# A pair's two heads: the six score products of an attention front multiplied in turn, head by head

## The chip, the cores and the metric

The kernel runs on one core of a Trainium2 chip. The metric is the device time of one execution in microseconds (us). Engines are named as in the profile: PE (TensorE, matrix products), PEld (its weight loads), DVE (VectorE), ACT (ScalarE), POOL (GpSimd), SP (the queue that issues the transfers).

## What is computed

One step of a hybrid encoder layer for 1024 prompt rows and 32 sample rows, width 2048, float32. One input projection feeds four branches; the change touches branch B, stick-breaking attention with 8 heads of width 64. For each block of 128 queries:

```python
z = jnp.einsum('bqhd,bkhd->bhqk', qblk, k).astype(jnp.float32) * scale
mask = (k_pos[None, :] < pblk[:, None])[None, None]
log_keep = jnp.where(mask, jax.nn.log_sigmoid(-z), 0.0)
suffix = lax.cumsum(log_keep, axis=3, reverse=True) - log_keep
w = jnp.where(mask, jnp.exp(jax.nn.log_sigmoid(z) + suffix), 0.0)
return jnp.einsum('bhqk,bkhd->bqhd', w, v32)
```

## The kernel before

The 1024 prompt rows are worked in two halves, h = 0 (with the 32 sample rows) and h = 1. The input projection goes through 48 column tiles of 128 (`col_tile`, L363 to L365): a tile `ip` is summed over 16 slices, with three products each, because a float32 operand is split into a high and a low part (`wh`, `wl` for weights, `uh`, `ul` for the input). A product streams 272 or 274 columns in half 0 and 512 in half 1 (256 twice where a half is cut in two). Weights come by SP (`wr`), ACT casts the high part (L338), DVE subtracts the low part (L339).

Branch B works on four pairs of heads, p = 0 to 3, in `b_unit`. A pair's q and k lie transposed in one tile each: head j = 0 in partitions 0 to 63, head j = 1 in 64 to 127. After the projections of q, k and v it runs 4 fronts in half 0 (query blocks i = 0 to 3 against the keys of this half up to the diagonal: 256, 256, 384 and 512 columns) and 8 in half 1 (the same four, and for each query block one more against the 512 keys of half 0, `prev`). That is 16 + 32 = 48 fronts. A front computes, for each of the two heads, the scores `z` as three products (high by high L737, high by low L738, low by high L739), each of which contracts over the head's 64 rows: on the array this is the form 64*128, where the projection has 128*128. Then `stick` lets ACT take two sigmoids of `z` (`s` L709, `kp` L710); POOL masks the diagonal block; DVE scans `kp` and multiplies (L718, L722). A later turn transposes the weights on PE (`turned`, `wt` L834) and multiplies them by the values (`values`, `av` L849, form 128*64).

`z` lies in PSUM in a pool of two buffers, so that a front's first head takes the buffer of the last front's first head and may be written when ACT's `kp` of that head is done; likewise the second head.

What runs around a front is set in two places. Python generators are woven: after so many steps of a projection tile, the next step of an attention unit is written out (`weave`, the table `ORDER`). Then a scheduler lists each engine's instructions in a fixed order, by its own estimate of when operands and buffers are ready; work under `tc.high_priority()` goes ahead of other work that is ready. `behind(a, b)` binds instruction a to stand behind b on its engine, without a wait. Engines carry out their list in this order.

Of the kernel before, what the change touches and what calls it, by code (L numbers as in the profile page):

```python
# [13 lines left out]
P = 128  # L14
# [48 lines left out]
def step_kernel(ctx, tc, xp, xs, cst, wmss, wmg, bgate, win, wsm, wout, lng, lnb, ck, cv,  # L63
# [19 lines left out]
    def nm(s):  # L83
        uid[0] += 1
        return f"{s}_{uid[0]}"

    def IO(s="io"):
        return io.tile([P, SLOT], F32, tag="io", name=nm(s))

    def WK(s="wk", shape=None):  # L90
        return wk.tile(shape or [P, SLOT], F32, tag="wk", name=nm(s))

    def ZT(s="z"):
        return ps_z.tile([P, 512], F32, tag="z", name=nm(s))
# [16 lines left out]
    T = nc.tensor  # L111
# [85 lines left out]
    def behind(ins, other):  # L197

        if other is not None:
            tc.add_manual_dep(ins.ins, other.ins.name, mybir.DependencyInfo(  # L200
                mybir.DependencyClass.NoSync, mybir.DependencyReason.DATA), reason="order")
        return ins
# [501 lines left out]
    def stick(z, rows, nk, diag, carry):  # L704


        s = WK("s")
        kp = WK("kp")
        A.activation(s[0:rows, 0:nk], z, AF.Sigmoid, scale=QSCALE)  # L709
        A.activation(kp[0:rows, 0:nk], z, AF.Sigmoid, scale=-QSCALE)  # L710
        if diag is not None:
            diag(s, kp)
        pr = WK("pr")
        init = 1.0
        if carry is not None:
            A.copy(pr[0:rows, nk:nk + 1], carry[0:rows, 0:1])
            init = carry[0:rows, 0:1]
        V.tensor_tensor_scan(pr[0:rows, 0:nk][:, ::-1], kp[0:rows, 0:nk][:, ::-1], kp[0:rows, 0:nk][:, ::-1],  # L718
                             initial=init, op0=ALU.mult, op1=ALU.bypass)

        m = nk - 1 if carry is None else nk
        V.tensor_tensor(s[0:rows, 0:m], s[0:rows, 0:m], pr[0:rows, 1:m + 1], op=ALU.mult)  # L722
        return s, pr
# [3 lines left out]
    def parts(t, name, n=512):  # L727

        th = io.tile([P, 512], F32R, tag="io", name=nm(name + "h"))
        tl = io.tile([P, 512], F32R, tag="io", name=nm(name + "l"))  # L730
        A.copy(th, t[:, 0:n])
        V.tensor_tensor(tl, t[:, 0:n], th.bitcast(F32), op=ALU.subtract)
        return th, tl

    def products(out, x, y, start, stop):

        T.matmul(out, x[0], y[0], start=start, stop=False)  # L737
        T.matmul(out, x[0], y[1], start=False, stop=False)  # L738
        T.matmul(out, x[1], y[0], start=False, stop=stop)  # L739
# [14 lines left out]
    def b_unit(h, p):  # L754
        n = 544 if h == 0 else 512
        tt = {}
        for name, tid in (("q", T_Q + p), ("k", T_K + p), ("v", T_V + p)):
            res = yield from col_tile(h, tid)
            t = IO(name)
# [11 lines left out]
        qs, ks_ = parts(q, "q"), parts(k, "k")  # L771
# [26 lines left out]
        if h == 1:  # L798
            prev_ = []
            for src in (ksc, vsc):  # L800
                t = (WK if src is ksc else IO)("prev")
# [4 lines left out]
        def front(i, st, kk, m, dg):  # L806

            def diag(s, kp):
                b = slice(i * P, (i + 1) * P)
                G.affine_select(out=s[:, b], in_=s[:, b], pattern=[[-1, P]], compare_op=ALU.is_gt,  # L810
                                fill=0.0, base=0, channel_multiplier=1)
                G.affine_select(out=kp[:, b], in_=kp[:, b], pattern=[[-1, P]], compare_op=ALU.is_gt,  # L812
                                fill=1.0, base=0, channel_multiplier=1)

            w = []
            for j in range(2):
                d = slice(64 * j, 64 * j + 64)
                z = ZT("z")
                products(z[:, 0:max(m, 256)], [t[d, i * P:(i + 1) * P] for t in qs],
                         [t[d, 0:max(m, 256)] for t in kk], True, True)  # L820
                wj, st[j] = stick(z[:, 0:m], P, m, diag if dg else None, st[j])
                w.append(wj)
            return w

# [33 lines left out]
        for i in range(4):  # L858
            st = [None, None, None]
            keys = [(ks_, vt, P * (i + 1), True)]  # L860
            if h == 1:
                keys.append((*prev_, 512, False))
            for x, (kk, vv, m, dg) in enumerate(keys):
                w = front(i, st, kk, m, dg)
                if todo2:
                    values(*todo2)
                    todo2 = None
                if todo1:
                    todo2 = (*todo1[:2], turned(todo1[2], todo1[4]), *todo1[3:])
                todo1 = (i, st, w, vv, m, x == 0, x == len(keys) - 1)  # L870
                yield 1
# [774 lines left out]
```

## Time and profile before

| | |
|---|---|
| time, median of 3 runs | 1991.29 us (1990.73 to 1994.05) |
| the profiled execution, its own time | 1989.37 us |
| its span, first to last instruction | 1987.6 us |
| mean granted TensorE clock | 0.984 |
| PE busy | 1901.5 us |
| DVE busy | 1338.2 us |
| ACT busy | 773.8 us |

The page gives the busy time of each engine over the span, and the views give single instructions with start and length. Matrix products overlap on PE, so the length of one says less than the distance from its start to the start of the next; that distance is called a step below. The rows of the timeline merge instructions of one line that follow each other (x2 is two of them).

### The profile page before, as it was taken

How to read it: one execution, taken by the hardware profiler on the slowest of the kernel's cores; microseconds unless marked ns; L12 is line 12 of the kernel's file. 1: busy time of each engine (PE TensorE's matmuls, PEld its weight loads, DVE VectorE, ACT ScalarE, POOL GpSimd, SP SyncE). 2: the span in 40 equal slices, each digit the busy share in tenths (PEclk: the TensorE clock that was granted, in tenths of full speed). 3: DMA queues.
4: the chain of work that ended last, by engine and by line, in shares of the span. 5: the costliest groups of instructions: out<-in, count | busy, mean ns of one | idle time of the engine just before them, and what ended most of it. 6: DMA issues, size and time to landing. Idle time of an engine off the chain costs nothing. (4 is left out here: it accounts for less than half of the span.)

```text
span 1987.6 us, 31999 instructions
## 1 busy us (share of the span) xinstructions
PE 1901.5 (96%) x12194; PEld 1578.5 (79%) x12194; DVE 1338.2 (67%) x2573; ACT 773.8 (39%) x1288; POOL 301.2 (15%) x505
## 2 busy tenths in 40 slices
PE   4999999999999999999999999999999999998997
PEld 2678999998898999876788786777878667676787
DVE  4425577977967858777677969875756653455765
ACT  5212433334564434544444444433345421133321
POOL 1100112212112202441101102021113310000000
PEclk9899999999999999998999999999999999999998
DMA  9787344333453343633233332332334554557633
GB/s 344 249 290 235 105 127 136 111 125 119 146 166 121 104 130 98 183 130 114 95 114 100 103 126 68 117 111 94 126 102 141 162 167 138 172 182 238 212 129 133
DMA packets 162098, 291.42 MB, mean 147 GB/s; under 512 B 23900, under 2 KB 66140, under 8 KB 161944
## 3 DMA queue, kind: packets, MB, share of 16 engines
q1 hardware_dynamic: 161944, 289.37, 45.2%
q8 instruction: 96, 1.57, 0.3%
q14 instruction: 58, 0.48, 0.1%
HBM read 253.49 MB, written 35.82 MB: 146 GB/s over the span
## 5 line engine op out<-in xcount | busy, mean ns | idle before, releaser
L363 PE MATMUL ip<-uh,wh 128*128 128x272 f32 (+3 forms) x2304 | 759.1, 330 | 0.7 <-POOL uh L288 0.7
L364 PE MATMUL ip<-ul,wh 128*128 128x272 f32 (+3 forms) x2304 | 747.4, 324 | 0.0
L365 PE MATMUL ip<-uh,wl 128*128 128x272 f32 (+3 forms) x2304 | 745.7, 324 | 0.0
L338 ACT CAST wh<-wr 128x1024 fp32r<-128x1024 f32 x253 | 264.0, 1044 | 635.3 <-PE ip L364 362.9
L339 DVE TENSOR_TENSOR wl<-wr,wh 128x1024 fp32r<-128x1024 f32 x253 | 312.1, 1235 | 240.1 <-ACT wh L338 222.5
L363 PEld LDWEIGHTS ip<-uh,wh 128*128 128x128 f32 x2304 | 438.7, 190 | 42.0 <-issue 9.6
L365 PEld LDWEIGHTS ip<-uh,wl 128*128 128x128 f32 x2304 | 438.2, 190 | 35.7 <-issue 4.5
L364 PEld LDWEIGHTS ip<-ul,wh 128*128 128x128 f32 x2304 | 438.2, 190 | 32.9 <-issue 4.3
L1256 PE MATMUL op<-wh,yh 128*128 128x512 f32 (+1 forms) x576 | 216.6, 376 | 7.8 <-DVE val L1267 7.8
L1258 PE MATMUL op<-wh,yl 128*128 128x512 f32 (+1 forms) x576 | 216.5, 377 | 0.0
L1257 PE MATMUL op<-wl,yh 128*128 128x512 f32 (+1 forms) x576 | 215.5, 374 | 0.0
L1118 DVE SCALAR_TENSOR_TENSOR cv<-cin,cs,cv 128x574 f32<-128x574 f32 (+1 forms) x240 | 187.5, 781 | 2.8
L1256 PEld LDWEIGHTS op<-wh,yh 128*128 128x128 f32 x576 | 109.4, 190 | 31.4 <-DVE val L1267 8.6
L1258 PEld LDWEIGHTS op<-wh,yl 128*128 128x128 f32 x576 | 109.3, 190 | 26.8 <-issue 7.2
L1257 PEld LDWEIGHTS op<-wl,yh 128*128 128x128 f32 x576 | 109.4, 190 | 24.0 <-issue 4.4
L1171 DVE SCALAR_TENSOR_TENSOR gacc<-wg,cs,gacc 128x512 f32<-128x512 f32 x120 | 91.6, 783 | 14.7 <-DMA wg<-in_wmg_dram 14.6
L810 POOL TENSOR_SCALAR_AFFINE_SELECT s<-s 128x128 f32<-128x128 f32 x64 | 37.9, 592 | 417.5 <-ACT s L709 417.1
L718 DVE TENSOR_TENSOR_SCAN pr<-kp 128x128 f32<-128x128 f32 (+4 forms) x66 | 53.9, 816 | 15.5 <-POOL kp L812 12.7
L213 PE MATMUL mod<-wmr,cpad 128*32 128x512 f32 x256 | 40.0, 703 | 25.2 <-DMA wmr<-in_wmss_dram 25.2
L709 ACT ACTIVATE s<-z 128x512 f32<-128x512 f32 (+3 forms) x96 | 47.7, 497 | 36.2 <-PE z L739 34.4
L722 DVE TENSOR_TENSOR s<-s,pr 128x512 f32<-128x512 f32 (+5 forms) x106 | 59.2, 562 | 2.1 <-DVE pr L718 0.5
L1072 POOL TENSOR_TENSOR dn<-dn,mhalf 128x1 f32<-128x1 f32 (+1 forms) x36 | 27.8, 771 | 211.6 <-DVE dn L1071 207.9
(384 smaller groups left out, 2333.2 us busy)
## 6 DMA issues: line engine op xcount, KB each, us to landing
wr<-in_win_dram SPq DMA_DIRECT2D x192, 512.0 KB
wmr<-in_wmss_dram SPq DMA_DIRECT2D x128, 256.0 KB
wr<-in_wout_dram SPq DMA_DIRECT2D x63, 512.0 KB
wg<-in_wmg_dram SPq DMA_DIRECT2D x64, 256.0 KB
x<-in_xp_dram SPq DMA_DIRECT2D x32, 256.0 KB
out_dram<-val SPq DMA_DIRECT2D x32, 256.0 KB
xr<-in_xp_dram SPq DMA_DIRECT2D x28, 256.0 KB
yf<-ysc SPq DMA_DIRECT2D x16, 272.0 KB
```

The costliest lines, as they stand in the source:

```text
L338: A.copy(wh, wr)
L339: V.tensor_tensor(wl, wr, wh.bitcast(F32), op=ALU.subtract)
L363: T.matmul(pt[:, 0:n], wh[:, k % 8, :], uh[:, c0:c0 + n], start=(k == 0), stop=False)
L364: T.matmul(pt[:, 0:n], wh[:, k % 8, :], ul[:, c0:c0 + n], start=False, stop=False)
L365: T.matmul(pt[:, 0:n], wl[:, k % 8, :], uh[:, c0:c0 + n], start=False, stop=(k == KD - 1))
L718: V.tensor_tensor_scan(pr[0:rows, 0:nk][:, ::-1], kp[0:rows, 0:nk][:, ::-1], kp[0:rows, 0:nk][:, ::-1], initial=init, op0=ALU.mult, op1=AL ...
L722: V.tensor_tensor(s[0:rows, 0:m], s[0:rows, 0:m], pr[0:rows, 1:m + 1], op=ALU.mult)
L1118: V.scalar_tensor_tensor(acc[:, 0:n], t[:, i:i + n], C("cdw", 31 * j + i), acc[:, 0:n], op0=ALU.mult, op1=ALU.add)
L1171: V.scalar_tensor_tensor(acc[j][:, 0:512], wr[:, 0:512], cT[:, k, j:j + 1], acc[j][:, 0:512], op0=ALU.mult, op1=ALU.add)
L1256: T.matmul(acc[t][:, 0:w], yh[:, c], wh, start=(first and i == 0), stop=False)
L1257: T.matmul(acc[t][:, 0:w], yh[:, c], wl, start=False, stop=False)
L1258: T.matmul(acc[t][:, 0:w], yl[:, c], wh, start=False, stop=(last and i == len(ws) - 1))
```

## The change

Before, `front` took a `z` buffer for head 0, issued its three products and its `stick`, then did the same for head 1. Now it takes both buffers first, then issues six products in the order high by high of head 0, of head 1, high by low of head 0, of head 1, low by high of head 0, of head 1. Each is bound behind the one before it, and the six stand under high priority. The two `stick` calls follow. The products themselves, their sizes and the number of buffers are the same.

```diff
+            zs = [ZT("z") for _ in range(2)]
+            n = max(m, 256)
+            after = None
+            with tc.high_priority():
+                for x, (a, b) in enumerate(((0, 0), (0, 1), (1, 0))):
+                    for j in range(2):
+                        d = slice(64 * j, 64 * j + 64)
+                        after = behind(T.matmul(zs[j][:, 0:n], qs[a][d, i * P:(i + 1) * P], kk[b][d, 0:n],
+                                                start=x == 0, stop=x == 2), after)
             w = []
             for j in range(2):
-                d = slice(64 * j, 64 * j + 64)
-                z = ZT("z")
-                products(z[:, 0:max(m, 256)], [t[d, i * P:(i + 1) * P] for t in qs],
-                         [t[d, 0:max(m, 256)] for t in kk], True, True)
-                wj, st[j] = stick(z[:, 0:m], P, m, diag if dg else None, st[j])
+                wj, st[j] = stick(zs[j][:, 0:m], P, m, diag if dg else None, st[j])
                 w.append(wj)
             return w
```

The lists of the engines change with it. First PE in half 1, second pair, the front i = 2 against its own half's keys; before, the six products stood in one piece between the end of a projection tile and the values of an older front:

```order
L365 MATMUL ip_12032<-uh_9968,wl_12023 128x512
L737 MATMUL z_12057<-kh_11665,qh_11661 128x384
L738 MATMUL z_12057<-kl_11666,qh_11661 128x384
L739 MATMUL z_12057<-kh_11665,ql_11662 128x384
L737 MATMUL z_12072<-kh_11665,qh_11661 128x384
L738 MATMUL z_12072<-kl_11666,qh_11661 128x384
L739 MATMUL z_12072<-kh_11665,ql_11662 128x384
L849 MATMUL av_12087<-wt_11982,vt_11675 64x128 x4
```

In this list the head (z_12057, z_12072) changes once. The same front on PE's list of the changed kernel, where L823 is the line of all six products:

```order
L364 MATMUL ip_11917<-ul_9929,wh_11907 128x512
L823 MATMUL z_12057<-kh_11665,qh_11661 128x384
L365 MATMUL ip_11917<-uh_9928,wl_11908 128x512
L363 MATMUL ip_11917<-uh_9936,wh_11907 128x512
L364 MATMUL ip_11917<-ul_9937,wh_11907 128x512
L365 MATMUL ip_11917<-uh_9936,wl_11908 128x512
L823 MATMUL z_12058<-kh_11665,qh_11661 128x384
L823 MATMUL z_12057<-kl_11666,qh_11661 128x384
L823 MATMUL z_12058<-kl_11666,qh_11661 128x384
L823 MATMUL z_12057<-kh_11665,ql_11662 128x384
L823 MATMUL z_12058<-kh_11665,ql_11662 128x384
L363 MATMUL ip_11917<-uh_9944,wh_11907 128x512
```

The heads alternate; the front stands earlier, inside an older projection tile; and one product of the first head stands alone, four projection products ahead of the other five.

The second place is PE in half 0, second pair, the front i = 1. Before, it stood in one piece between the transposes of another unit (`xt`) and those of an older front (`wt`):

```order
L365 MATMUL ip_3213<-uh_908,wl_3157 128x272
L317 MATMUL xt_3276<-ident,xk_3101 128x128 x4
L737 MATMUL z_3284<-kh_3014,qh_3010 128x256
L738 MATMUL z_3284<-kl_3015,qh_3010 128x256
L739 MATMUL z_3284<-kh_3014,ql_3011 128x256
L737 MATMUL z_3299<-kh_3014,qh_3010 128x256
L738 MATMUL z_3299<-kl_3015,qh_3010 128x256
L739 MATMUL z_3299<-kh_3014,ql_3011 128x256
L834 MATMUL wt_3314<-ident,s_3119 128x128
```

Now five of the six stand inside the projection tile `ip_3160`, which comes earlier on the list:

```order
L363 MATMUL ip_3160<-uh_698,wh_3156 128x274
L823 MATMUL z_3285<-kh_3014,qh_3010 128x256
L823 MATMUL z_3284<-kl_3015,qh_3010 128x256
L823 MATMUL z_3285<-kl_3015,qh_3010 128x256
L823 MATMUL z_3284<-kh_3014,ql_3011 128x256
L823 MATMUL z_3285<-kh_3014,ql_3011 128x256
L364 MATMUL ip_3160<-ul_699,wh_3156 128x274
```

The sixth, high by high of `z_3284`, stands nine projection products further ahead in the same tile, 16 projection products behind the four transposes `xt_3107`.

Over the whole of PE's list the 288 score products stood in 51 unbroken runs (45 of six) and now stand in 96: 38 of one, 38 of five, 10 of two, 10 of four. On ACT's list the sigmoids keep their places but for those of the first front. On SP's list 18 transfers change places with a neighbour; most are weight loads `wr` that stand one place later.

## Rows read from the trace of the kernel before

**Rows 1.** The page: busy us (share of the span) and instructions of each engine.

```profile
PE 1901.5 (96%) x12194; PEld 1578.5 (79%) x12194; DVE 1338.2 (67%) x2573; ACT 773.8 (39%) x1288; POOL 301.2 (15%) x505
```

**Rows 2.** Windows, the two stretches with attention fronts: busy us by engine, granted clock, DMA.

```profile
205.00:480.00 275.00, 269.41 (x2174) 258.29 (x2175) 205.16 (x393) 101.06 (x182) 49.02 (x79) 0.99 0.38 120
900.00:1250.00 350.00, 341.37 (x2005) 265.31 (x2003) 276.02 (x401) 161.62 (x302) 43.53 (x69) 0.99 0.32 102
```

**Rows 3.** Tile z: line, engine, operation, count, ns least/median/most, forms.

```profile
L739 PE MATMUL z<-kh,ql x64: 272/306/394, 208.1 to 1232.3; 64*128 64x256 f32 x32, 64*128 64x384 f32 x16, 64*128 64x512 f32 x16
L739 PE MATMUL z<-prevh,ql x32: 383/392/393, 930.6 to 1241.8; 64*128 64x512 f32 x32
```

**Rows 4.** Timeline of PE, half 1, a front with both heads: start us, length us, instruction.

```profile
1045.96 0.40 PE L365 MATMUL ip<-uh,wl 128*128 128x512 f32 x1
1046.29 0.45 PE L737 MATMUL z<-kh,qh 64*128 64x384 f32 x2
1046.57 0.34 PE L738 MATMUL z<-kl,qh 64*128 64x384 f32 x2
1046.74 0.34 PE L739 MATMUL z<-kh,ql 64*128 64x384 f32 x2
1047.02 0.66 PE L849 MATMUL av<-wt,vt 128*64 128x128 f32 x8
```

**Rows 5.** Timeline of PE, half 1, one head's three products alone.

```profile
1218.23 0.39 PE L365 MATMUL ip<-uh,wl 128*128 128x512 f32 x1
1218.46 0.39 PE L363 MATMUL ip<-uh,wh 128*128 128x512 f32 x1
1218.78 0.45 PE L737 MATMUL z<-kh,qh 64*128 64x384 f32 x1
1219.07 0.33 PE L738 MATMUL z<-kl,qh 64*128 64x384 f32 x1
1219.24 0.33 PE L739 MATMUL z<-kh,ql 64*128 64x384 f32 x1
1219.51 0.49 PE L364 MATMUL ip<-ul,wh 128*128 128x512 f32 x1
1219.84 0.40 PE L365 MATMUL ip<-uh,wl 128*128 128x512 f32 x1
1220.08 0.40 PE L363 MATMUL ip<-uh,wh 128*128 128x512 f32 x1
```

**Rows 6.** Timeline of PE, half 0, a front between transposes and a projection tile.

```profile
283.97 0.60 PE L317 MATMUL xt<-ident,xk 128*128 128x128 f32 x4
284.50 0.40 PE L737 MATMUL z<-kh,qh 64*128 64x256 f32 x2
284.72 0.29 PE L738 MATMUL z<-kl,qh 64*128 64x256 f32 x2
284.84 0.29 PE L739 MATMUL z<-kh,ql 64*128 64x256 f32 x2
285.06 0.40 PE L363 MATMUL ip<-uh,wh 128*128 128x274 f32 x1
285.29 0.29 PE L364 MATMUL ip<-ul,wh 128*128 128x274 f32 x1
285.42 0.29 PE L365 MATMUL ip<-uh,wl 128*128 128x274 f32 x1
```

**Rows 7.** Waits of PE from 205 to 480 us: us in total, times, longest.

```profile
PE av L849 <- ACT wt L837: 2.8, 1, 2.8
PE av L849 <- DVE yb L854: 0.9, 1, 0.9
```

**Rows 8.** Waits of PE from 900 to 1250 us.

```profile
PE av L849 <- DVE yb L854: 2.2, 3, 1.0
PE wt L834 <- DVE s L722: 2.1, 5, 0.8
```

**Rows 9.** Timeline of ACT behind the front of rows 6.

```profile
286.29 0.29 ACT L710 ACTIVATE kp<-z 128x128 f32<-128x128 f32 x1
```

## The prediction

> **What bounds the kernel now.** I read the page first, for the engine that has no time to spare: PE is busy for 1901.5 us of the span, 96%, and no other compute engine comes near [rows 1]. Then the windows over the two stretches in which attention fronts run: PE is busy for 269.4 of 275 us and for 341.4 of 350 us, at a granted clock of 0.99, which is the upper level of 2.4 GHz almost throughout [rows 2]. Only 5.6 + 8.6 = 14.2 us there are not PE's. DVE, the next, has 70 and 74 us to spare. So whatever the change adds to PE's own time in these stretches goes into the span, and what it saves comes out of it. The tile's view gives the work at stake: 96 products in the third line, so 288 in all, and 64 rows of the array in each [rows 3]. The list of before has the second head's three products behind the first head's; the timeline shows what PE makes of that.
>
> **What alternating saves: nothing.** In a front with both heads the timeline has the products in pairs, x2 in each line, that is both heads' high by high together, then both heads' high by low, and so on. From the last projection product before to the first instruction behind, it takes 1047.02 - 1045.96 = 1.06 us [rows 4]. One head's three products of the same size, alone on PE, take 1219.51 - 1218.46 = 1.05 us from product to product [rows 5]. The second head is free already: with the list head by head, the two halves of the array work side by side, and six products take three slots. Alternating can't make three slots fewer, since each head has three products in a row on its own half.
>
> One rule says otherwise. The Trainium skill, page "TensorE: Matmul & The Clock Gate", Part 3, states that products start and end strictly in program order. By that, the six of before would have run one behind the other, and alternating would halve them. The trace does not agree: the line of the second head's first product is merged with that of the first head's, ahead of two products that stand before it on the list. What the rule would make of the time is the first rival.
>
> **What the change costs: changes of the array's form.** The same rows give the price of going from 128*128 to 64*128 and back. In half 1 a projection step is 0.23 us (1218.23 to 1218.46); the step into the score product is 0.32, so +0.09. The second score product starts 0.29 behind the first, the third 0.17 behind the second: +0.12. The step out is 0.27 against a slot of 0.17: +0.10. The second projection product then starts 0.33 behind the first, against 0.24 for the next: +0.09 [rows 5]. In half 0 the same four prices appear: the second score product 0.22 against 0.12, the step out 0.22 against 0.12, and behind it 0.23 against 0.13 [rows 6]. So each change of form costs about 0.1 us at once and another 0.1 us at the second product behind it, if one follows.
>
> Now the count, from PE's whole lists before and after. Changes of form rise from 479 to 602, by 123. Of these, 75 are returns to 128*128, with a projection behind them: 75 x 0.20 = 15.0 us. Another 48 are entries into a form of few rows or columns (47 into 64*128, 1 into 128*64): 48 x 0.10 = 4.8 us. I count only the first half of the price for these, since a run of one product has no second, and since the run that keeps three slots paid its second half before as well. Part of the 75 comes from fronts that went straight on into `av`, as in rows 4, and now have projection products between.
>
> Then the single products. Where a front is split into one and five, the one uses a slot of its own with half the array empty, and the five still need three slots, because all three of the second head are among them. A slot is 0.12 us at 256 columns [rows 6] and 0.17 at 384 [rows 5]; at 512 I estimate 0.22 on the same line. Of the 38 singles, 12 are in half 0, four each of 256, 384 and 512 columns: 4 x 0.51 = 2.0 us. In half 1 there are 14 against the older keys, 512 columns each, and four each of the other three sizes: 14 x 0.22 + 2.0 = 5.1 us. Together 7.1. The ten fronts split into two and four keep three slots. On the credit side, before has one front in half 1 in which the heads ran apart, one of them in rows 5; its second three slots, 3 x 0.17 = 0.5 us, fall away, and about 0.3 for a first front in half 0 that was cut up in the same way. The sum is 15.0 + 4.8 + 7.1 - 0.8 = 26.1 us.
>
> **What the earlier place may save or cost.** The scores are ready earlier, and PE's waits for what follows from them could shrink: for `av` and `wt` it waited 2.8 + 0.9 us in the first stretch [rows 7] and 2.2 + 2.1 in the second [rows 8], 8.0 us in all. The bounds are 0 and 8.0. On ACT's list, though, the sigmoids keep their places, so most of what comes after them is no earlier. I take 2.
>
> Against that, PE now comes to a front's first product about when its buffer is free. The one case that rows allow me to check is in half 0. The projection product after the four transposes would start at 283.97 + 4 x 0.11 = 284.41 (the four start 0.53 us ahead of the score product, of which 0.09 is the step in); with 16 projection products of 0.13 us and the step in, the front's next first product falls at 286.58. The `kp` that frees its buffer ended at 286.29 + 0.29 = 286.58 [rows 6, 9]. A tie, so a wait of perhaps 0.1 us. I take 0.05 us for each of the 48 fronts, 2 us, and this cancels the gain. The bounds are 0, and half a microsecond each, 24 us. Behind such a wait stands the projection on PE's list, and behind that the evacuations on ACT and DVE. The 18 transfers that swap places on SP I take at nothing: their cover is that PE's waits in both stretches name no weight load. If that cover goes, the wait would be named `ip` behind `wl`; no row prices it, and I leave a few us at the upper end.
>
> POOL, DVE and ACT get the same instructions as before. The sum against the profiled execution's own time, 1989.4 us, is 1989.4 + 26.1 = 2015.5. That execution lies 1.9 us under the median of the runs, so between 2015 and 2018; I say **2016 us**, about 1.2% slower.
>
> **The rivals.**
>
> First, the rule of order in practice: the pairs of before are not really side by side, and the change saves slots. One slot of all 48 fronts is 4 x 0.61 us in half 0 (0.12 twice, 0.17, 0.22) and 4 x (0.61 + 4 x 0.22) in half 1, 8.4 us. Six slots would become three, saving 25.2; the singles take 7.1 back and the changes of form 19.8. That is 1.7 us slower, 1993 us, no change that can be told. Against it stand rows 4 and 5 with their equal lengths. Chance 0.04.
>
> Second, on the other side: PE is not what paces these stretches, but the weights that DVE and ACT prepare. Then PE's extra work disappears in time it would have waited, while the waits for `av` and `wt` go: 1991.3 - 8.0 = 1983 us. For it speaks that DVE is busy for three quarters of both stretches. It decides only from the point at which PE has as much idle time as the 26 us it is given; it has 14.2 us [rows 2]. Chance 0.06, with all other ways of being faster.
>
> Third, much slower: the first products wait for ACT. If ACT runs half a microsecond behind the scheduler's plan in every front, PE stops 48 times, for 24 us, and the time is 2040 us. For it: the list puts the product at the moment at which the plan frees the buffer, so any lateness of ACT is PE's. Against it: the tie above, and that the second head's first product stands four projection products of 0.23 us, or nine of 0.13, further on. Chance 0.10.
>
> The rest, 0.80, is the forecast.
>
> **The range.** The low end takes the changes of form at 0.1 us each with no second half, 12.3 + 6.3, and all 8.0 us of waits gone: 10.6 us, 2002. The high end takes all 123 at 0.2 us with the singles, 31 us, and 8 us of waits and late loads: 2030. A difference of 0.2%, 4 us, is about what a measurement of this kernel can tell from no change. So faster (under 1987) 0.06, within it 0.05 (the first rival and one in a hundred of the forecast), slower 0.89.
>
> **What the profile of the changed kernel would show.** Right: a timeline in which single score products stand between projection products, the step in about 0.1 us longer than the normal one, the step out and the next one as well; fives that take as long as the sixes of before; PE busy for 20 to 30 us more over the two stretches, with idle time there as before. Score products x2 in the timeline both before and after. Wrong in the first step: a front of five or six that takes clearly less time than 1.06 us at 384 columns in half 1. Wrong in the price: changes of form as counted, but projection products that follow them at their normal step, so that the loss is under 10 us. Wrong on the waits: rows in which PE's `z` waits for ACT's `kp`, more than a few us in all. I would also be wrong if PE's idle time in the two stretches fell by much more than 8 us.

## The result, and the profile after

The changed kernel takes 2014.84 us (median of 4 runs, 2010.58 to 2017.48). The kernel before, run beside it, takes 1991.34 us. The ratio is 1.0105 with a 95% interval of 1.0076 to 1.0133, so it is slower by 21 us, between 15 and 26 (the two medians are 23.5 us apart). The profiled execution takes 2013.76 us, with a span of 2012.0 us.

The page of the changed kernel, busy us of each engine, answers to [rows 1]:

```profile
PE 1929.6 (96%) x12194; PEld 1581.3 (79%) x12194; DVE 1338.6 (67%) x2573; ACT 772.2 (38%) x1286; POOL 301.9 (15%) x505
```

The number of products is the same, and PE is busy for 1929.6 - 1901.5 = 28.1 us more. PEld has 2.8 us more, and no other engine gained as much as 1. Where the loss is, is seen best between points of the same work. I take the stretch from the 161st to the 741st of the products `ip<-uh,wh` of L363 (the fronts of half 0), and from the 1501st to the 2001st (all fronts of half 1). One front is not in both: the first of half 0 stands at 207.7 us in before, inside the stretch, and at 182.1 in the changed kernel, ahead of it. These are the windows over the two stretches in before, and over two shorter ones in which its granted clock was at the lower level; columns as in [rows 2]:

```profile
193.96:462.38 268.42, 265.57 (x2139) 254.18 (x2139) 198.48 (x388) 102.10 (x183) 45.44 (x73) 1.00 0.39 124
857.81:1300.32 442.51, 430.38 (x2503) 338.19 (x2502) 346.68 (x547) 200.53 (x365) 62.20 (x88) 0.98 0.32 104
918.91:929.15 10.24, 9.81 (x30) 6.77 (x30) 4.84 (x23) 4.25 (x8) 0.00 (x0) 0.50 0.19 57
1284.14:1290.97 6.83, 6.11 (x15) 4.86 (x16) 6.58 (x18) 0.27 (x1) 0.20 (x1) 0.50 0.22 78
```

And the windows over the same work in the changed kernel:

```profile
197.00:473.03 276.03, 274.77 (x2134) 257.29 (x2133) 199.90 (x389) 100.18 (x182) 44.61 (x77) 1.00 0.38 120
865.66:1322.76 457.10, 446.58 (x2505) 337.33 (x2503) 344.03 (x545) 201.70 (x365) 66.07 (x89) 0.99 0.31 101
930.70:934.11 3.41, 3.41 (x10) 2.59 (x10) 1.56 (x7) 3.38 (x7) 0.00 (x0) 0.50 0.29 89
1309.58:1312.99 3.41, 3.39 (x9) 2.71 (x10) 3.41 (x13) 0.27 (x1) 0.00 (x0) 0.50 0.46 154
```

The reader is to take three differences from these eight rows.

- The stretches are longer by 276.03 - 268.42 = 7.61 and 457.10 - 442.51 = 14.59 us, together 22.2 of the 24.4 us that the span grew.
- PE's idle time (length less busy) goes from 2.85 to 1.26 and from 12.13 to 10.52 us. It falls by 3.2.
- A clock of 0.50 is the level of 1.2 GHz, at which a step of 512 columns takes 0.43 us (1058.67 to 1059.10 in the rows of "The early place in one piece" below) and not 0.23. PE was busy at that level for 9.81 + 6.11 = 15.92 us and now is for 3.41 + 3.39 = 6.80. I take half of the difference, 4.6 us, as time that the clock gave back; by these two steps it would be 4.2.

So PE's own work at full clock grew by 22.2 + 3.2 + 4.6 = 30.0 us. This estimate is the figure against which the prediction's sum must be read, and the table behind the experiments has it for every kernel. The rest of the span is -2.8 us between the two stretches, where there are no fronts, and +5.0 us outside all three.

The timeline of PE in the changed kernel, the front of [rows 4], shows what that work is:

```profile
1041.58 0.41 PE L363 MATMUL ip<-uh,wh 128*128 128x512 f32 x1
1041.82 0.40 PE L364 MATMUL ip<-ul,wh 128*128 128x512 f32 x1
1042.15 0.44 PE L823 MATMUL z<-kh,qh 64*128 64x384 f32 x1
1042.52 0.50 PE L365 MATMUL ip<-uh,wl 128*128 128x512 f32 x1
1042.86 0.40 PE L363 MATMUL ip<-uh,wh 128*128 128x512 f32 x1
1043.09 0.39 PE L364 MATMUL ip<-ul,wh 128*128 128x512 f32 x1
1043.32 0.39 PE L365 MATMUL ip<-uh,wl 128*128 128x512 f32 x1
1043.64 0.44 PE L823 MATMUL z<-kh,qh 64*128 64x384 f32 x1
1043.64 0.61 PE L823 MATMUL z<-kl,qh 64*128 64x384 f32 x2
1043.92 0.50 PE L823 MATMUL z<-kh,ql 64*128 64x384 f32 x2
1044.35 0.50 PE L363 MATMUL ip<-uh,wh 128*128 128x512 f32 x1
1044.69 0.40 PE L364 MATMUL ip<-ul,wh 128*128 128x512 f32 x1
```

The five take 1044.35 - 1043.32 = 1.03 us from product to product, as the six did: 1.06 us. The single one ahead of them comes on top. Its step in is 0.33 us, its step out 0.37, the next 0.34; two plain steps of 0.23 would stand there without it. It costs 1.04 - 0.46 = 0.58 us, a slot of 0.17 and 0.41 more. The five take no fewer slots than the six did, so alternating saved none.

The weight loads in the same front show one thing more about a change of form:

```profile
1041.58 0.19 PEld L364 LDWEIGHTS ip<-ul,wh 128*128 128x128 f32 x1
1042.52 0.19 PEld L365 LDWEIGHTS ip<-uh,wl 128*128 128x128 f32 x1 [0.18 <-issue]
1043.64 0.18 PEld L823 LDWEIGHTS z<-kh,qh 64*128 64x128 f32 x1 [0.36 <-issue]
```

The first load starts a step ahead of its product (1041.82). The other two stand behind a change of form and start together with theirs. So it is in all 186 changes between 128*128 and 64*128 in this trace (products of 256 columns or more, outside waits and the lower clock): the load starts within 3 ns of its product, where between products of one form it mostly starts 0.11 to 0.24 us ahead. A load that nothing covers fits the 0.10 us on the step behind the first product; no run tests this reading.

The waits of PE in the changed kernel from 205 to 490 us (us in total, times, longest), against [rows 7]:

```profile
PE av L855 <- DVE yb L860: 1.6, 1, 1.6
...
PE z L823 <- ACT kp L710: 0.2, 1, 0.2
```

And from 900 to 1275 us, against [rows 8]:

```profile
PE z L823 <- ACT kp L710: 2.2, 2, 1.4
PE wt L840 <- DVE s L722: 1.1, 2, 1.0
...
PE av L855 <- DVE yb L860: 0.2, 1, 0.2
```

The waits for `av` and `wt` named in [rows 7, 8] went from 8.0 to 2.9 us, and the new wait, that of a front's first product for the buffer that `kp` frees, is 2.4 us. The two terms that the prediction set against each other were -2 and +2.

### The profile page after: what moved, and what is told of

It is laid out like the page before. It is cut to its first block, busy times and chain, and to the rows that moved or that the text cites. A ratio compares the mean times of both kernels' runs of the same rounds, so it can differ in the third digit from the quotient of the medians.

```text
span 2012.0 us, 31990 instructions
## 1 busy us (share of the span) xinstructions
PE 1929.6 (96%) x12194; PEld 1581.3 (79%) x12194; DVE 1338.6 (67%) x2573; ACT 772.2 (38%) x1286; POOL 301.9 (15%) x505
## 5 line engine op out<-in xcount | busy, mean ns | idle before, releaser
L363 PE MATMUL ip<-uh,wh 128*128 128x272 f32 (+3 forms) x2304 | 759.0, 330 | 0.7 <-POOL uh L288 0.7
L363 PEld LDWEIGHTS ip<-uh,wh 128*128 128x128 f32 x2304 | 438.0, 190 | 43.0 <-issue 12.3
L810 POOL TENSOR_SCALAR_AFFINE_SELECT s<-s 128x128 f32<-128x128 f32 x64 | 45.1, 705 | 426.8 <-ACT s L709 426.5
L843 ACT COPY wt<-wt 128x512 f32<-128x512 f32 (+1 forms) x80 | 40.8, 549 | 72.6 <-PE wt L840 70.2
L718 DVE TENSOR_TENSOR_SCAN pr<-kp 128x128 f32<-128x128 f32 (+4 forms) x66 | 54.0, 818 | 15.5 <-POOL kp L812 12.9
```

What stands on the lines that cost most here:

```text
L363: T.matmul(pt[:, 0:n], wh[:, k % 8, :], uh[:, c0:c0 + n], start=(k == 0), stop=False)
```

## The experiments

Each is given with its ratio to before, run beside it on the same chip (median 1995.54 us for the first four, 1993.35 for the last two).

**Alternating alone.** The changed kernel without the high priority: six products in turn, each bound behind the last, at the place where the scheduler puts them by itself.

```diff
-            with tc.high_priority():
-                for x, (a, b) in enumerate(((0, 0), (0, 1), (1, 0))):
...
+            for x, (a, b) in enumerate(((0, 0), (0, 1), (1, 0))):
...
```

> The heads in turn, but without the priority: 52 unbroken runs of score products (51 before, 96 in the change) and 481 changes of the array's form (479 and 602). My theory, that the loss is the changes of form and the slots of the single products: 1991 us, within 4 of before. Rival order (multiplying in turn itself costs): 2014 us, as the change. Rival strict order (in before the two heads ran one after the other, and the change saved slots that the changes of form ate): about 25 us faster than before, 1966 us. Rival place (the early place makes PE wait for ACT): 1991 us, as mine; the third run tells these two apart.

Measured: 1993.81 us, ratio 0.9985 (0.9969 to 1.0001). No change that can be told. PE's busy time is 1901.8 us, as before. By itself, multiplying the heads in turn has no worth and no cost that can be told. The loss of the change is all in what the priority does to the list. With six slots made three the ratio would have been about 0.987.

**The place without the alternation.** The changed kernel with its two loops exchanged: both buffers first, high priority, bound, but head by head.

```diff
-                for x, (a, b) in enumerate(((0, 0), (0, 1), (1, 0))):
-                    for j in range(2):
+                for j in range(2):
+                    for x, (a, b) in enumerate(((0, 0), (0, 1), (1, 0))):
```

> Priority and both buffers at once as in the change, but the products listed head by head: 98 runs, 74 of them of three products of one head, and 610 changes of form. My theory: changes of form cost as in the change, about 24 us, and in 37 fronts the heads stand apart and take six slots for three, 37/48 of 25.2 = 19 us, where the change lost 7 for its singles: about 2027 us, 2020 to 2036. Rival strict order: the number of slots is that of before, so only the changes of form are paid, 2010 us. Rival place: as the change, 2014 us.

Measured: 2029.64 us, ratio 1.0165 (1.0144 to 1.0185), 33 us slower. The heads now stand apart on the list, and each pays for itself. The timeline of PE in this kernel, one head of a front of 384 columns (the other follows at 956.92):

```profile
955.23 0.39 PE L364 MATMUL ip<-ul,wh 128*128 128x512 f32 x1
955.55 0.44 PE L823 MATMUL z<-kh,qh 64*128 64x384 f32 x1
955.83 0.34 PE L823 MATMUL z<-kl,qh 64*128 64x384 f32 x1
956.00 0.34 PE L823 MATMUL z<-kh,ql 64*128 64x384 f32 x1
956.27 0.50 PE L365 MATMUL ip<-uh,wl 128*128 128x512 f32 x1
```

Three products take 956.27 - 955.23 = 1.04 us, what five take in the changed kernel and six in before. Given the early place, then, the alternation does help: it keeps five together where the other order cuts the front into three and three.

**The early place in one piece.** The changed kernel, with the first product made to wait also for the last `kp` and the last low part that were written out, so that nothing has to be waited for between it and the other five.

```diff
-        A.activation(kp[0:rows, 0:nk], z, AF.Sigmoid, scale=-QSCALE)
+        late[0] = A.activation(kp[0:rows, 0:nk], z, AF.Sigmoid, scale=-QSCALE)
...
-                        after = behind(T.matmul(zs[j][:, 0:n], qs[a][d, i * P:(i + 1) * P], kk[b][d, 0:n],
-                                                start=x == 0, stop=x == 2), after)
+                        mm = T.matmul(zs[j][:, 0:n], qs[a][d, i * P:(i + 1) * P], kk[b][d, 0:n],
+                                      start=x == 0, stop=x == 2)
+                        for o in () if after else late:
+                            if o is not None:
+                                tc.add_manual_dep(mm.ins, o.ins.name, mybir.DependencyInfo(
+                                    mybir.DependencyClass.Sync, mybir.DependencyReason.DATA), reason="order")
+                        after = behind(mm, after)
```

> The change with its early place, but the first product also waits for what frees the second buffer and for the last low part, so that all 48 fronts stand in one piece of six: 48 runs, 501 changes of form. My theory: 22 more changes than before at 0.2 us, less what early scores give back: 1994 us, 1987 to 1999. Rival place (the early place and its waits cost): near the change, 2008 us or more. Rival order: 2014 us.

Measured: 2007.76 us, ratio 1.0055 (1.0035 to 1.0074), 11 us slower; the expectation missed. All 48 fronts stand in one piece, so the singles are gone. The timeline of PE shows what came instead, in half 1:

```profile
1054.03 0.39 PE L365 MATMUL ip<-ul,wh 128*128 128x512 f32 x1
1058.08 0.79 PE L824 MATMUL z<-kh,qh 64*128 64x512 f32 x2 [3.65 <-ACT kp L711]
1058.67 0.62 PE L824 MATMUL z<-kl,qh 64*128 64x512 f32 x2
1059.10 0.63 PE L824 MATMUL z<-kh,ql 64*128 64x512 f32 x2
```

The front stands where the plan thinks that both heads' buffers are free, and ACT is 3.65 us later. The rows of ACT and DVE show that it is not ACT that is slow:

```profile
1050.31 4.69 DVE L1130 SCALAR_TENSOR_TENSOR cv<-cin,cs,cv 128x512 f32<-128x512 f32 x6
1056.05 1.28 DVE L719 TENSOR_TENSOR_SCAN pr<-kp,pr 128x512 f32<-128x512 f32 x1
1057.43 0.60 ACT L711 ACTIVATE kp<-z 128x512 f32<-128x512 f32 x1 [4.02 <-DVE pr L719]
```

ACT stands idle for 4.02 us ahead of the second head's `kp`, until DVE's scan `pr` is done, and that scan stands behind six `cv` operations (4.69 us) and a low part (`wl`). It happens twice (3.67 us the second time, at 1154.39, with five `cv` ahead of the scan). Each time the clock drops before the wait is over: 0.50 from 1057.21 to 1064.04 us, and again from 1152.78 to 1159.61. In the second stretch PE's idle time is 20.4 us, not 12.1, and its busy time at the lower level 21.4 us, not 15.9. PE's own work is up by 3.6 us only (table below). So the third rival's mechanism is real where the first product waits for both heads' buffers. In the change it waits for one, and the other five follow when the second is free: the split that costs changes of form seems to cover this wait as well, which its waits of 2.4 us fit but no run shows by itself.

**One row half for both heads.** The kernel before with the second head reading the first head's 64 rows, so that the second head's scores are those of the first. This takes away what would let two products run side by side.

```diff
             for j in range(2):
-                d = slice(64 * j, 64 * j + 64)
+                d = slice(0, 64)
```

> The kernel before, with the second head's products reading the first head's 64 rows (the second head's scores are then those of the first). The list is that of before. My theory (in before the two heads run side by side on the two halves of the array): now six slots in a row, 8.4 us for each slot position, so 25 us more, about 2016 us, 2008 to 2022. Rival strict order (they ran one after the other anyway): no change, 1991 us.

Measured: 2007.31 us, ratio 1.0061 (1.0037 to 1.0085), 12 us slower; half of what was expected. The timeline of PE, the front of 384 columns, shows the mechanism whole:

```profile
960.16 0.40 PE L365 MATMUL ip<-uh,wl 128*128 128x512 f32 x1
960.50 0.44 PE L737 MATMUL z<-kh,qh 64*128 64x384 f32 x1
960.78 0.33 PE L738 MATMUL z<-kl,qh 64*128 64x384 f32 x1
960.95 0.33 PE L739 MATMUL z<-kh,ql 64*128 64x384 f32 x1
961.12 0.33 PE L737 MATMUL z<-kh,qh 64*128 64x384 f32 x1
961.30 0.33 PE L738 MATMUL z<-kl,qh 64*128 64x384 f32 x1
961.47 0.34 PE L739 MATMUL z<-kh,ql 64*128 64x384 f32 x1
961.74 0.66 PE L849 MATMUL av<-wt,vt 128*64 128x128 f32 x8
```

Six steps, none merged: 961.74 - 960.16 = 1.58 us, against 1.06 in [rows 4]. So before did have two heads at a time. PE's own work grew by 24.9 us, as the slots say; 13 us of it did not reach the time. In the profiled execution PE idles less (6.78 us in the second stretch, not 12.13) and spends less of it at the lower clock; how far the clock's part is the kernel's is taken up below.

**More singles, nothing else early.** The changed kernel with only the first product of each front under high priority.

```diff
             with tc.high_priority():
...
+                after = product(0, 0, 0, 0)
+            for x, a, b, j in ((0, 0, 0, 1), (1, 0, 1, 0), (1, 0, 1, 1), (2, 1, 0, 0), (2, 1, 0, 1)):
+                after = behind(product(x, a, b, j), after)
```

> The heads in turn, only the first product of each front under the priority; the other five stand where the front stood before. 48 single products, 569 changes of form (479 before, 602 in the change). My theory: each single costs 0.4 us of changes (the trace of the change has 0.09 into it, 0.21 over its slot out of it, 0.10 at the second product behind) and its slot, so 48 x 0.4 + 8.4 = 28 us on PE, less some 9 us that waits and the slower clock give back, as they did in the change: 19 us over before, 10 to 27. Rival place (it is the early scores and the waits for ACT that cost): five of six products are where they were, so within 4 us of before.

Measured: 2011.21 us, ratio 1.0078 (1.0053 to 1.0104), 15.5 us slower. Five of six products are back at the place that the scheduler chooses, and most of the loss stays. It goes with the single product, of which there are 48 here and 38 in the change.

**Scores that keep the projection's form.** The kernel before with high and low part of a head's q stacked in 128 rows, and high (then low) part of k doubled in 128 rows. Two products over 128 rows take the place of three over 64, and the scores no longer change the array's form. It adds low by low, which before leaves out, and 44 more instructions each on ACT and DVE.

```diff
-                products(z[:, 0:max(m, 256)], [t[d, i * P:(i + 1) * P] for t in qs],
-                         [t[d, 0:max(m, 256)] for t in kk], True, True)
+                n = max(m, 256)
+                T.matmul(z[:, 0:n], qs[j][:, i * P:(i + 1) * P], kk[j][0][:, 0:n], start=True, stop=False)
+                T.matmul(z[:, 0:n], qs[j][:, i * P:(i + 1) * P], kk[j][1][:, 0:n], start=False, stop=True)
```

> The kernel before, with the high and low part of a head's q stacked in 128 rows and k's high part, and its low part, twice: a head's scores are two products over 128 rows in place of three over 64, so a front is four products and no change of form on its account; it adds the low by low product. 56 entries into 64*128 at 0.2 us and 29 returns at 0.2 us go, 17 us; one slot more in each front, 8.4 us; so 9 us less on PE. ACT and DVE get 4 more half-height operations per pair in half 0 and 7 in half 1, some 30 us in all, inside their idle time. My theory: 4 to 9 us faster than before, 0.2 to 0.45%. Rival (the extra slots and the work on DVE and ACT cost what the changes of form save, or these don't cost 0.2 us): no change, or up to 10 us slower.

Measured: 1990.75 us, ratio 0.9972 (0.9953 to 0.9991): 5.6 us faster than before by the ratio, between 2 and 9; the medians are 2.6 us apart. The timeline of PE, a front of 256 columns:

```profile
1017.61 0.39 PE L365 MATMUL ip<-uh,wl 128*128 128x512 f32 x1
1017.84 0.28 PE L836 MATMUL z<-kh,qh 128*128 128x256 f32 x1
1017.96 0.28 PE L837 MATMUL z<-kl,qh 128*128 128x256 f32 x1
1018.08 0.28 PE L836 MATMUL z<-kh,qh 128*128 128x256 f32 x1
1018.20 0.28 PE L837 MATMUL z<-kl,qh 128*128 128x256 f32 x1
1018.32 0.40 PE L363 MATMUL ip<-uh,wh 128*128 128x512 f32 x1
1018.55 0.39 PE L364 MATMUL ip<-ul,wh 128*128 128x512 f32 x1
```

The steps in, out and next are the plain 0.23, 0.12 and 0.23. The front takes 0.71 us where it took 0.89 before (the same pair's, at 1011.78), although it has four slots for three. At 384 columns with `av` behind it, it is 1.03 against 1.06. At 512 it depends on what follows: behind the front, `av` changes the form all the same, and it is 1.25 against 1.22; with a projection there, 1.16 against 1.24. Its profiled execution is no faster than that of before (span 1990.2 us); PE's idle time between the two stretches is 3.7 us longer there. The gain rests on the ratio over 12 and 17 runs alone.

**The bill for all of them.** Changes of form are counted between successive products in each trace. Slots are score products that don't start together with the product before them (56 - 48 of 256 columns more in the changed kernel, 32 - 27 of 384, 95 - 72 of 512), at 0.12, 0.17 and 0.22 us each. In the stacked kernel every score product is a slot. The bill takes 0.20 us for each change of form, 0.10 at the change and 0.10 one step on. The column of PE's work is over the two stretches, worked out from one profile each as in the first section; the last column is from all runs.

| kernel | changes of form | slots, us | bill, us | PE's work, us | time by the ratio, us |
|---|---|---|---|---|---|
| before | 500 | 26.2 | | | |
| changed | +123 | +6.9 | 31.5 | 30.0 | +21 |
| alternating alone | +2 | -0.3 | 0.1 | 0.4 | -3 |
| place, head by head | +131 | +22.4 | 48.6 | 46.5 | +33 |
| early, in one piece | +22 | -0.5 | 3.9 | 3.6 | +11 |
| one row half | 0 | +25.0 | 25.0 | 24.9 | +12 |
| first product early | +90 | +7.6 | 25.6 | 25.0 | +15.5 |
| stacked | -69 | +8.1 | -5.7 | -4.4 | -5.6 |

Two prices from a few rows of before account for PE's work in seven kernels to within 3 us. In three of them (changed, head by head, in one piece) the first front has moved ahead of the stretches, so the work column lacks it; counted within the stretches their bills are 29.9, 46.9 and 3.1 us. What the prices don't account for is how much of the work becomes time. Here the two last columns must be set against each other with care: before's profiled execution, at 1989.37 us, lies 6 and 4 us below the medians of its runs in these experiments, and each work figure is a difference from that one.

## Why the prediction came out as it did

**Alternating saves nothing: right.** It is shown from both sides, by alternating alone (no change) and by one row half for both heads (six slots in a row, 1.58 us). The rule in the Trainium skill, page "TensorE: Matmul & The Clock Gate", Part 3, that products start and end strictly in program order, does not hold here between products on different row halves. With it, the second head's first product could at best have gone beside the first head's last, and the six of before would have taken five steps; they took three (1.06 us against 1.05 for three alone). Nor does PE start its products in the order of its list, as the section on the kernel has it. The first rival falls with this. Its sum has a slip that changes nothing: 0.12 twice, 0.17 and 0.22 are 0.63 and not 0.61, so one slot of all fronts is 8.6 us and not 8.4.

**The count of form changes: right.** Forecast 123 more, and the trace has 623 - 500 = 123.

**The price of one: under-sized by 4.8 us.** The step that failed is "I count only the first half of the price for these, since a run of one product has no second". It has one. The second 0.10 us falls on the step behind the first product after a change, whatever comes there; if the run ends with that product, this is the step out. In the changed kernel's rows above, the single's step out is 0.37 us, where a run of five has 0.26 (its last product starts at 1044.09) and one of three 0.27 (head by head). So all 123 changes cost 0.20 us, 24.6 and not 15.0 + 4.8 = 19.8. I had priced from [rows 4 to 6], where every run has a second product.

**The singles' slots: right to 0.6 us.** Forecast 7.1 less 0.8 of credit, 6.3, counted 6.9.

**Waits and clock: the size was off, in the other direction.** The prediction let saved and new waits cancel, and gave the clock no term. PE's idle time fell by 3.2 us in the two stretches and the lower clock's share by 4.6. So the sum was 4 us too low in work (26.1 against 30.0; 5 by the bill of 31.5) and 8 us too high in what becomes time, and the rest of the span grew by 2.2. That 2016 us came out so close to 2014.84 is luck in part: the errors have opposite signs. Of the 8 us, the idle time belongs to the change as far as one profile each can tell: three more kernels in which PE got some 25 us or more (head by head, one row half, first product early) also have less idle time in the second stretch, 6.2, 6.8 and 8.8 us against 12.1. That slower fronts leave DVE and ACT more time is the likely reason, but was only argued. The clock's part is in good part chance. Alternating alone has 8.5 us at the lower level in that stretch, not 15.9, with a list that is nearly that of before. The mean granted clock of before's 35 executions beside the experiments runs from 0.981 to 0.991, with a mean of 0.986; the changed kernel's four have 0.987 to 0.989, with a mean of 0.988. The two profiled executions, at 0.984 and 0.989, are further apart than that, so a part of the 4.6 us, by these means about half, belongs to those two executions and not to the kernels. Whether the rest is the change's own stays open.

**The second rival** (PE not the pace, 1983 us) needed as much idle time as PE was given work. It had 15.0 us in the two stretches and gave 3.2. It falls as a whole, but a part of it is in the four rows of the table in which PE got some 25 us or more.

**The third rival** (first products wait for ACT, 2040 us) did not happen: 2.4 us in three waits. The early-in-one-piece kernel shows a case in which it does, when the first product needs the second head's buffer as well; there DVE holds ACT up, and ACT holds PE up.

The loads on SP that changed places, set at nothing, show no wait of `ip` behind `wl` in the changed kernel's list of waits.

## What to carry to other kernels

Before two small products are put side by side by hand, look in the timeline whether their rows are merged (x2): on different row halves of the array they ran together here however the list had them, as long as they stood in one run, and then what counts is into how many runs the list cuts them. Each change of the array's form cost 0.2 us here, so a single small product between large ones cost 0.4 us and its slot. When priority pulls a group of products forward, look at the engine's list for what it tears apart, and correct a sum of added work for the waiting time that the engine still has.

## What had not been expected of the hardware

- The price of a change of form comes in two parts of 0.10 us, the second on the step behind the first product after it. At 256, 384 and 512 columns the step out of a single product is 0.31, 0.37 and 0.42 us in the changed kernel (medians of 8, 8 and 22), 0.2 above its slot in each case. The Trainium skill, page "TensorEngine Tiling (Array Packing)", section "Key Properties", says that changing the mode drains the engine. The trace agrees as far as it goes: each change costs time, and no weight load runs ahead across one. The 0.2 us is this case's figure for it.
- With both heads listed head by head, the second head's first product starts 0.010 us behind the first head's, ahead of two that stand before it on the list; listed in turn, it starts 0.003 us behind. That is all that the order changes.
- In each of the two waits of 3.65 and 3.67 us in the early-in-one-piece kernel the granted clock fell to 0.50, 0.9 and 1.6 us before the wait ended, and stayed there for 6.83 us. In before, 10.24 us at 0.50 begin while a wait of 2.5 us ends (`rt` for DVE's `w`), and in the changed kernel 3.41 us behind one of 2.9. The length at the lower level does not follow the length of the wait in these.
